# State space layer of a three-layer fp32 block: skip folded into the chunk matrices, a new order of states and outputs, and p @ w_pe of the next gate moved into it

## The chip, the cores and the metric

The kernel is one program on one core of a Trainium2 chip. The metric is device time in microseconds of one execution. Before the change three runs took 3111.47, 3125.9 and 3119.45 us, median 3119.45.

## What is computed

A sequence of 512 tokens with 1024 features passes through a first block (convolutions and gating, a mixture of experts, a gated embedding) and a second block of two layers. The first layer of the second block is a state space layer; it is followed by a feed-forward part and again by a gated embedding. The change touches the state space layer and that gated embedding:

```
def s5_mixer(h, w_in, ..., d_skip, w_glu):
    u = h @ w_in
    ...
    y = ys.transpose(2, 0, 1, 3, 4).reshape(bsz, seqlen, SSM_DIM)
    y = y + d_skip.astype(f32) * u.astype(f32)
    g = jax.nn.gelu(y).astype(h.dtype)
    val, gate = jnp.split(g @ w_glu, 2, axis=-1)
    return val * jax.nn.sigmoid(gate)
...
    x = x + conv_ffn(h, ffn_w_up[i], ffn_conv_w[i], ffn_conv_b[i], ffn_w_down[i])
    gate = jax.nn.sigmoid(rms_norm(x, ple_norm[i]) @ ple_w_gate[i])
    x = x + (p[i] @ ple_w_proj[i]) * gate
```

`ys` is a linear recurrence over time, with a complex diagonal state of 64 per group of 16 features (64 groups).

## The kernel before, in words

**Products.** Features lie on the 128 partitions, the 512 tokens along the free side; `x` is 8 tiles of 128x512. Every fp32 product is made of three passes of rounded operands (`mm3`, L161 to L163): high x high, low x high, high x low. Weights come as strips of 128 output features (512 KB, 128x1024). For a strip SP loads the raw tile (`wr`, L135), ACT makes the high part (`wh`, L148), DVE or POOL (if the strip's `pool` flag is set) subtracts for the low part (`wl`, L150), and PE does 24 matmuls of 128x512. An activation is split in the same way (ACT L117 or L119, DVE L112 or L114).

**Order.** No scheduler moves anything: each engine executes its instructions in the order in which the program calls them. `order` lists all strips of the kernel in the order of use. `next_strip` loads up to `LA_DMA` strips and prepares up to `LA` strips ahead of the one in use. `tick` ends an item of work; `later(n, f)` puts the work of the other engines on that item n items further on. All loads of strips and most other DMAs are issued from the one queue of SP, in order; an issue that waits (for a free buffer, or for data that it writes out) holds all that stand behind it. Raw strips have four buffers (`wr`), `wh` and `wl` three each.

**The state space stage** (`ssm`) works through the list `SSM_ORDER` of items for m = 0 to 7:

- `u m`: one strip of `ssm_w_in`. PE multiplies; DVE scales into `u` (L1470); SP writes it to DRAM (`ud`, L1471) and reads it back in another layout (`U`, L1465).
- `s m`: 32 small matmuls of the matrices `m2` with `U` (L1494, tile `st`). DVE multiplies twice by the table `csd` (L1502, L1503), POOL adds (L1504, L1505), DVE scans (L1511), multiplies twice (L1512, L1513), and DVE and POOL form the states `X` (L1520).
- `o m`: 32 matmuls (tile `yy`, L1530 and L1531) of `m1` with `U` and `m3` with `X`. ACT copies out (`y`, L1540, four pieces), PE turns the tile (`yt`, L1546), DVE adds the skip (L1551), ACT applies gelu (L1555), and the result is split into `yg` (ACT L117, DVE L112).

`m1`, `m2`, `m3` and `csd` are 512, 512, 512 and 256 KB per item, built earlier in the expert stage (`ssm_prep`) and read back from DRAM. Afterwards 16 strips of `w_glu` are multiplied with `yg`.

**The gated embedding** (`ple`) multiplies eight strips of `w_pg` with the normalised `x` and gates p @ w_pe with it: `w_pe` is two strips of four output tiles, each tile 6 matmuls (`pp`). `ple_head` does four tiles between the feed-forward part and the first gate strip, `ple_proj(1)` the other four between gate strips 5 and 6. `ple(i)` for i = 1 is the one after the feed-forward part of the state space layer.

## Time and profile before

| what | value |
|---|---|
| median of three runs | 3119.45 us |
| the profiled execution's own time | 3122.41 us |
| its span, first to last instruction | 3120.6 us |
| PE busy, DVE busy | 94%, 71% |
| ACT busy, POOL busy | 41%, 38% |
| mean granted clock of TensorE | 0.965 of full |
| state space stage, from the first u strip to the first w_glu strip | about 1786 to 1875 us of the span |
| gated embedding after it | about 2326 to 2392 us |

PE stands for matmuls, PEld for weight loads, POOL for GpSimd, SP for the queue that issues most transfers. Busy time of PE is a modelled overlap of pipelined matmuls; a stage is read better from when one group of matmuls starts and the next one starts. A row's bracket says how long the engine was idle before the instruction and what ended that.

### The profile page before, as it was taken

What the parts mean: (1) busy time and instruction counts of PE and PEld (TensorE: products, weight loads), DVE (VectorE), ACT (ScalarE), POOL (GpSimd) and SP (SyncE); (2) the same over time, 40 slices, a digit from 0 to 9 for tenths busy, and PEclk for the clock granted to TensorE, in tenths of its full rate; (3) what the DMA queues carried; (4) which work ended last, traced back from release to release, by engine and by line L of the source; (5) the groups of instructions that cost most, each with busy time, mean ns of one, the idle gap of its engine ahead of it and who ended that gap; (6) DMA issues with size and microseconds to landing.
All of it is one profiled execution on the core that took longest, in us unless ns stands there. A gap on an engine that the chain in (4) does not pass through costs nothing. (4 is left out here: it accounts for less than half of the span.)

```text
span 3120.6 us, 39487 instructions
## 1 busy us (share of the span) xinstructions
PE 2923.9 (94%) x14359; PEld 2456.2 (79%) x14359; DVE 2216.9 (71%) x3786; ACT 1266.7 (41%) x2016; POOL 1183.6 (38%) x1032
## 2 busy tenths in 40 slices
PE   8999988888999999999998989999999998999998
PEld 6677888787888787878877768888877766888886
DVE  7946888995898878787887684565675457566665
ACT  4333256566433333333334533433344345433333
POOL 3224565653248879788886330000011011100001
PEclk9889999999999999999999989999999989999999
DMA  4124344778788888888986283233332211233322
GB/s 138 48 84 150 105 142 163 248 252 305 252 290 304 291 314 299 307 286 305 317 291 221 89 256 103 86 101 98 97 97 88 81 40 49 93 97 101 95 73 96
DMA packets 248891, 534.77 MB, mean 171 GB/s; under 512 B 36671, under 2 KB 129219, under 8 KB 248314
## 3 DMA queue, kind: packets, MB, share of 16 engines
q1 hardware_dynamic: 170570, 343.69, 33.7%
q0 software_dynamic: 38656, 140.74, 13.0%
q10 hardware_dynamic: 39472, 47.84, 4.4%
q8 instruction: 113, 1.85, 0.2%
q14 instruction: 80, 0.66, 0.1%
HBM read 468.75 MB, written 63.44 MB: 171 GB/s over the span
## 5 line engine op out<-in xcount | busy, mean ns | idle before, releaser
L150 DVE TENSOR_TENSOR wl<-wr,wh 128x1024 fp32r<-128x1024 f32 (+2 forms) x453 | 548.7, 1221 | 456.4 <-ACT wh L148 447.6
L148 ACT ACTIVATE wh<-wr 128x1024 fp32r<-128x1024 f32 (+2 forms) x552 | 545.7, 997 | 505.5 <-PE mm L163 209.9
L161 PE MATMUL mm<-xn,wh 128*128 128x512 f32 x1296 | 521.4, 402 | 12.9 <-ACT xn L119 7.6
L163 PE MATMUL mm<-xn,wh 128*128 128x512 f32 x1296 | 512.4, 395 | 5.8 <-DVE xn L114 5.8
L162 PE MATMUL mm<-xn,wl 128*128 128x512 f32 x1296 | 512.8, 396 | 2.0 <-POOL wl L150 1.9
L230 POOL TENSOR_TENSOR accs<-accs,sq 128x512 f32<-128x512 f32 x56 | 86.2, 1540 | 1014.1 <-ACT sq L229 1009.2
L1077 PE MATMUL pv<-wh,A 128*128 128x512 f32 x1536 | 443.2, 402 | 22.5 <-DVE A L112 10.1
L150 POOL TENSOR_TENSOR wl<-wr,wh 128x1024 fp32r<-128x1024 f32 x99 | 241.1, 2436 | 450.4 <-ACT wh L148 439.4
L1077 PEld LDWEIGHTS pv<-wh,A 128*128 128x128 f32 x1536 | 291.8, 193 | 89.0 <-DVE A L112 17.6
L162 PE MATMUL mm<-n,wl 128*128 128x384 f32 x1024 | 348.3, 340 | 13.5 <-DVE wl L150 11.7
L161 PE MATMUL mm<-n,wh 128*128 128x384 f32 x1024 | 352.7, 344 | 0.8 <-ACT gs L703 0.8
L163 PE MATMUL mm<-n,wh 128*128 128x384 f32 x1024 | 347.8, 340 | 3.1 <-DVE n L114 3.1
L161 PEld LDWEIGHTS mm<-xn,wh 128*128 128x128 f32 x1296 | 248.6, 192 | 68.4 <-ACT xn L119 8.1
L163 PEld LDWEIGHTS mm<-xn,wh 128*128 128x128 f32 x1296 | 248.0, 191 | 61.4 <-DVE xn L114 8.6
L162 PEld LDWEIGHTS mm<-xn,wl 128*128 128x128 f32 x1296 | 248.6, 192 | 55.9 <-POOL wl L150 2.3
L1077 PE MATMUL pv<-wl,A 128*128 128x512 f32 x768 | 245.3, 401 | 26.6 <-DVE wl L150 26.6
L117 ACT ACTIVATE A<-ga 128x384 fp32r<-128x384 f32 x128 | 67.3, 525 | 424.6 <-DVE ga L1039 421.4
L998 DVE SCALAR_TENSOR_TENSOR gx<-gx,first 128x1024 f32<-128x1024 f32 x127 | 178.9, 1409 | 59.6 <-DMA gx<-in_exp_v,first 57.9
L162 PEld LDWEIGHTS mm<-n,wl 128*128 128x128 f32 x1024 | 196.0, 191 | 17.8 <-DVE wl L150 13.9
L161 PEld LDWEIGHTS mm<-n,wh 128*128 128x128 f32 x1024 | 196.0, 191 | 5.2 <-issue 1.6
L1077 PEld LDWEIGHTS pv<-wl,A 128*128 128x128 f32 x768 | 145.9, 192 | 67.4 <-DVE wl L150 35.1
L163 PEld LDWEIGHTS mm<-n,wh 128*128 128x128 f32 x1024 | 195.9, 191 | 3.5 <-DVE n L114 3.5
(409 smaller groups left out, 5356.4 us busy)
## 6 DMA issues: line engine op xcount, KB each, us to landing
wr<-in_exp_u SPq DMA_DIRECT2D x128, 512.0 KB
wr<-in_exp_v SPq DMA_DIRECT2D x128, 512.0 KB
wr<-in_w_up SPq DMA_DIRECT2D x88, 512.0 KB
gd<-gb ACTq DMA_DIRECT2D x48, 512.0 KB
G<-gd SPq DMA_DIRECT2D x32, 768.0 KB
wr<-in_w_dn SPq DMA_DIRECT2D x64, 320.0 KB
wr<-in_w_pg SPq DMA_DIRECT2D x24, 512.0 KB
sd<-gs SPq DMA_DIRECT2D x56, 192.0 KB
```

Source lines behind the costliest of these rows:

```text
L117: nc.scalar.activation(hi, src, AF.Copy)
L148: nc.scalar.activation(s.hi, s.raw, AF.Copy)
L150: eng.tensor_tensor(s.lo, s.raw, s.hi.bitcast(F32), ALU.subtract)
L161: t.matmul(ps, wh, xh, start=start, stop=False)
L162: t.matmul(ps, wl, xh, start=False, stop=False)
L163: t.matmul(ps, wh, xl, start=False, stop=stop)
L230: self.later(1, lambda: nc.gpsimd.tensor_tensor(acc, acc, sq, ALU.add))
L998: nc.vector.scalar_tensor_tensor(out=acc, in0=g, scalar=act[:, j : j + 1], in1=acc, op0=ALU.mult, op1=ALU.add)
L1077: nc.tensor.matmul(pv[2 * b + h], a[:, x, o], w[:, h * T : h * T + T], start=(e == 0 and i == 0 and w is s.hi), stop=last)
```

## The change

The skip `d_skip * u` is no longer added by DVE. It is added to the diagonal of the matrices `m1` when these are built: ACT copies only the part of the tile behind the first 16 columns, and DVE adds `eye * d` to the first 16 in two small instructions for each of the 16 parts. Gelu reads the turned tile in PSUM. The low part of `yg` is made by POOL. Outputs come later in the order (three states ahead), the lag of the turning matmuls is 2 items, and the strips of `u3` and `u5` get their low part from POOL.

The eight tiles of p @ w_pe for the gated embedding that follows are made inside the state space stage, as two items `p0` and `p1` of four tiles. ACT copies each tile out (`ppo`), SP writes it to DRAM (`ppd`, L1597 after the change), and `ple` reads the tiles back (`ppk`). The two strips of `w_pe` get their low part from POOL. Both places in the gated embedding where these matmuls stood fall away there.

```
     def plan_ple(self, i):
...
+        if i == 1:
+            self.order += g
+        else:
+            self.order += p[:1] + g[:6] + p[1:] + g[6:]
...
     def ple(self, after, kept=None):
...
+        def fetch(m):
+            if kept is not None and m < 8:
+                self.pp[m] = self.st.tile([P, T], F32, tag="ppk", name=self.name("ppk"), bufs=4)
+                nc.sync.dma_start(self.pp[m], kept[m])
...
         def gate(m):
+            fetch(m + 2)
...
-        for _ in self.ple_proj(1):
+        for _ in self.ple_proj(1) if kept is None else ():
...
-                nc.scalar.copy(o, pk[0:32])
+                nc.scalar.copy(o[:, :, 16:], pk[0:32, :, 16:])
+                for a in range(QP):
+                    V.scalar_tensor_tensor(
+                        out=o[:, a, 0:16], in0=eye, scalar=dT[:, q * QP + a : q * QP + a + 1], in1=pk[0:32, a, 0:16], op0=ALU.mult, op1=ALU.add
+                    )
...
-    YL = 1
+    YL = 2
...
-    SSM_ORDER = "u0 u1 u2 u3 s0 u4 s1 u5 o0 s2 u6 o1 s3 u7 o2 s4 o3 s5 o4 s6 o5 s7 o6 o7"
+    SSM_ORDER = "u0 u1 u2 u3 s0 u4 s1 u5 s2 o0 u6 s3 o1 u7 s4 o2 p0 s5 o3 s6 o4 s7 p1 o5 o6 o7"
...
-            def skip(m, ps):
-                y2 = self.tmp((P, 8, NCH), tag="y2")
-                nc.vector.scalar_tensor_tensor(
-                    out=y2, in0=u[m], scalar=self.v("ssm_d")[:, m : m + 1], in1=ps, op0=ALU.mult, op1=ALU.add
-                )
+            def bend(m, ps):
                 y = self.tmp(tag="yg")
-                nc.scalar.activation(y.rearrange("p (n t) -> p t n", t=8), y2, AF.Gelu_apprx_tanh)
-                self.split(yg[:, m, 0, :], yg[:, m, 1, :], y)
+                nc.scalar.activation(y.rearrange("p (n t) -> p t n", t=8), ps, AF.Gelu_apprx_tanh)
+                hi, lo = yg[:, m, 0, :], yg[:, m, 1, :]
+                nc.scalar.copy(hi, y)
+                self.later(1, lambda: nc.gpsimd.tensor_tensor(lo, y, hi.bitcast(F32), ALU.subtract))
+
+            def project(h):
+                s = self.next_strip()
+                for j in range(4):
+                    ps, m = self.mm(name="pp"), 4 * h + j
+                    for k in range(2):
+                        c = slice((2 * j + k) * P, (2 * j + k + 1) * P)
+                        self.mm3(ps, s.hi[:, c], s.lo[:, c], self.ph[:, k, 0, :], self.ph[:, k, 1, :], k == 0, k == 1)
+                    def keep(ps=ps, m=m):
+                        o = self.tmp(tag="ppo")
+                        nc.scalar.copy(o, ps)
+                        nc.sync.dma_start(ppd[m], o)
+                    self.later(1, keep)
+                    self.tick()
...
+            self.ple_fetch(1)
+            self.later(8, self.ple_load)
             stat(st)
-            la, self.LA_DMA = self.LA_DMA, self.SSM_LA
+            la, self.LA_DMA, self.LA = (self.LA_DMA, self.LA), self.SSM_LA, 3
...
-        self.ple_head()
+        if ple == 2:
+            self.ple_head()
```

**First place: SP's queue behind the write of u5.** `ud<-u` writes u5 and later u6 to DRAM, `m1d`, `m3d` and `m2d` are the chunk matrices, `in_ssm_w_in` is the strip of u7. Before:

```order
L1471 DMA ud<-u_2626_14995 128x512
L135 DMA wr_15354<-m2d 128x1024
L1479 DMA tab_14999<-csd 128x512
L135 DMA wr_15392<-in_ssm_w_in 128x1024
L1465 DMA U_15420<-ud 128x8x64
L135 DMA wr_15437<-m1d 128x8x128
L135 DMA wr_15443<-m3d 128x1024
L1471 DMA ud<-u_2627_14996 128x512
```

After the change the same stretch of SP's queue, up to the first strip of `w_pe`:

```order
L1500 DMA ud<-u_15387 128x512
L1508 DMA tab_15028<-csd 128x512
L135 DMA wr_15399<-m1d 128x8x128
L135 DMA wr_15401<-m3d 128x1024
L135 DMA wr_15437<-in_ssm_w_in 128x1024
L1493 DMA U_15465<-ud 128x8x64
L135 DMA wr_15471<-m2d 128x1024
L1500 DMA ud<-u_15499 128x512
L1508 DMA tab_15028<-csd 128x512
L135 DMA wr_15511<-m1d 128x8x128
L135 DMA wr_15513<-m3d 128x1024
L135 DMA wr_15551<-in_w_pe 128x1024
```

The strip of u7 stood behind one matrix (m2 of s3) and the table; it now stands behind the two matrices of o1 and the table. The matrices of o2 stood ahead of the write of u6 and now stand behind it.

**Second place: SP's queue from the last read of U to the second strip of w_pe.** `ppd<-ppo` writes one tile of p @ w_pe. Before, from the write of u7:

```order
L1471 DMA ud<-u_2628_14997 128x512
L135 DMA wr_15582<-m1d 128x8x128
L1479 DMA tab_14999<-csd 128x512
L135 DMA wr_15619<-m3d 128x1024
L135 DMA wr_15621<-m2d 128x1024
L1465 DMA U_15640<-ud 128x8x64
L135 DMA wr_15663<-m1d 128x8x128
```

After the change, from the last read of U; the write of the last tile of p0 is the one that ends in 15720:

```order
L1493 DMA U_15674<-ud 128x8x64
L1597 DMA ppd<-ppo_15677 128x512
L1597 DMA ppd<-ppo_15696 128x512
L1597 DMA ppd<-ppo_15709 128x512
L1597 DMA ppd<-ppo_15720 128x512
L135 DMA wr_15723<-m1d 128x8x128
L1508 DMA tab_15028<-csd 128x512
L135 DMA wr_15751<-m3d 128x1024
L135 DMA wr_15753<-m2d 128x1024
L135 DMA wr_15788<-in_w_pe 128x1024
```

The matrices of o4 followed the last read of U directly; they now stand behind four writes that wait for the tiles of p0, and the matrix of s7 and the strip of p1 stand behind those.

**Third place: the end of the stage, SP and ACT.** `in_w_glu` are the strips that follow the stage. SP before:

```order
L135 DMA wr_15778<-m3d 128x1024
L135 DMA wr_15780<-m1d 128x8x128
L135 DMA wr_15820<-m3d 128x1024
L135 DMA wr_15855<-in_w_glu 128x1024
L135 DMA wr_15857<-in_w_glu 128x1024
```

SP after the change:

```order
L1597 DMA ppd<-ppo_15944 128x512
L1597 DMA ppd<-ppo_15954 128x512
L135 DMA wr_15957<-m1d 128x8x128
L135 DMA wr_15959<-m3d 128x1024
L135 DMA wr_15984<-in_w_glu 128x1024
L135 DMA wr_15990<-in_w_glu 128x1024
L135 DMA wr_16019<-in_w_glu 128x1024
```

ACT after the change, from the last copy of o6 (`y_16010`) to the first gelu of the last three:

```order
L1569 COPY y_16010<-yy_15992 64x4x4x16
L148 ACTIVATE wh_16015<-wr_15990 128x1024
L148 ACTIVATE wh_16021<-wr_16019 128x1024
L1569 COPY y_16053<-yy_16027 64x4x4x16
L1569 COPY y_16054<-yy_16027 64x4x4x16
L1569 COPY y_16053<-yy_16027 64x4x4x16
L1569 COPY y_16054<-yy_16027 64x4x4x16
L1580 ACTIVATE yg_16068<-yt_16044 128x8x64
```

The last matrices (o7) and the strips of `w_glu` now stand behind the writes of the four tiles of p1, and on ACT the copies of o7 stand behind the high parts of the second and third strip of `w_glu`.

## Rows read from the trace of the kernel before

**Rows 1.** The page, chain that ended last: share of the span by engine.

```profile
PE 34%; DVE 5%; issue 1%; ACT 1%; POOL 0%; DMA 0%; SPq 0%; ACTq 0%; POOLq 0%; DVEq 0%
```

**Rows 2.** Windows: us, busy us of PE, PEld, DVE, ACT, POOL; PEclk, DMA share, GB/s.

```profile
1800.00:1820.00 20.00, 17.39 (x153) 14.37 (x152) 17.83 (x22) 4.66 (x8) 8.11 (x12) 0.91 0.74 214
1820.00:1840.00 20.00, 19.19 (x189) 15.75 (x188) 17.30 (x23) 8.29 (x15) 6.77 (x12) 0.92 0.92 275
1840.00:1860.00 20.00, 13.13 (x207) 12.38 (x208) 16.92 (x24) 9.57 (x19) 7.82 (x15) 0.83 1.03 320
1860.00:1876.00 16.00, 11.03 (x92) 9.57 (x93) 12.60 (x16) 7.12 (x14) 4.81 (x7) 0.57 0.57 209
```

**Rows 3.** Groups of DVE from 1797 to 1876: count, busy us, mean ns, idle before.

```profile
L112 DVE TENSOR_TENSOR yg<-yg,yg 128x512 fp32r<-128x512 f32 x6 | 5.8, 964 | 0.1
L1551 DVE SCALAR_TENSOR_TENSOR y<-u,vec,yt 128x512 f32<-128x512 f32 x7 | 5.2, 736 | 1.5 <-PE yt L1546 1.5
```

**Rows 4.** Timeline of DVE: start, us, instruction; idle time before in brackets.

```profile
1827.80 1.23 DVE L150 TENSOR_TENSOR wl<-wr,wh 128x1024 fp32r<-128x1024 f32 x1 [0.89 <-ACT wh L148]
...
1829.55 1.19 DVE L1470 TENSOR_TENSOR u<-mm,rstd 128x512 f32<-128x512 f32 x1
```

**Rows 5.** Timeline of SP: start, us, and the transfer issued.

```profile
1819.24 0.32 SPq L1471 DMA_DIRECT2D ud<-u  x1
...
1820.57 0.42 SPq L135 DMA_DIRECT2D wr<-in_ssm_w_in  x1
```

**Rows 6.** Timeline of ACT: start, us, idle time before in brackets.

```profile
1785.68 0.58 ACT L254 COPY rstd<-px 128x512 f32<-128x512 f32 x1 [1.66 <-PE px L252]
...
1826.71 1.06 ACT L148 ACTIVATE wh<-wr 128x1024 fp32r<-128x1024 f32 x1 [2.46 <-DMA wr<-in_ssm_w_in]
...
1873.39 1.29 ACT L1540 COPY y<-yy 64x256 f32<-64x256 f32 x4 [3.52 <-PE yy L1531]
```

**Rows 7.** Timeline of PE in the state space stage.

```profile
1810.88 0.45 PE L1530 MATMUL yy<-wr,U 128*64 128x128 f32 x4
...
1812.68 1.15 PE L1494 MATMUL st<-U,wr 128*64 128x64 f32 x32
...
1816.44 1.11 PE L1546 MATMUL yt<-ident,y 64*128 64x64 f32 x8 [2.61 <-ACT y L1540]
...
1829.62 0.50 PE L161 MATMUL mm<-xn,wh 128*128 128x512 f32 x1
...
1861.88 0.44 PE L1531 MATMUL yy<-wr,X 128*64 128x128 f32 x1 [0.80 <-POOL X L1520]
...
1869.68 0.45 PE L1531 MATMUL yy<-wr,X 128*64 128x128 f32 x1 [4.11 <-POOL X L1520]
...
1875.12 0.50 PE L161 MATMUL mm<-yg,wh 128*128 128x512 f32 x1
```

**Rows 8.** Tile wl on POOL, whole kernel: ns shortest, median, longest; first and last start.

```profile
L150 POOL TENSOR_TENSOR wl<-wr,wh x99: 2333/2398/3215, 21.5 to 2634.7; 128x1024 fp32r<-128x1024 f32 x99
```

**Rows 9.** Timeline of PE in the gated embedding after the feed-forward part.

```profile
2326.16 0.50 PE L161 MATMUL pp<-ph,wh 128*128 128x512 f32 x1
...
2343.32 0.95 PE L240 MATMUL px<-ones,accs 128*128 128x1 f32 x8
...
2369.28 0.40 PE L161 MATMUL pp<-ph,wh 128*128 128x512 f32 x1
...
2374.56 0.39 PE L163 MATMUL pp<-ph,wh 128*128 128x512 f32 x1
```

**Rows 10.** Timeline of DVE there.

```profile
2332.28 1.72 DVE L150 TENSOR_TENSOR wl<-wr,wh 128x1024 fp32r<-128x1024 f32 x1
...
2336.22 1.62 DVE L114 SCALAR_TENSOR_TENSOR xn<-x,vec,xn 128x512 fp32r<-128x512 f32 x2
```

**Rows 11.** Where m1 is built: tile m1o, and the timeline of ACT behind it.

```profile
L1375 ACT COPY m1o<-m1p x16: 344/346/362, 941.6 to 1680.3; 32x256 f32<-32x256 f32 x16
...
942.99 1.06 ACT L148 ACTIVATE wh<-wr 128x1024 fp32r<-128x1024 f32 x1 [1.06 <-issue]
```

More of the change, by code (lines that the diff above doesn't have):

```diff
@@ L1120, in ple_head, with ple @@
             pass
-    def ple(self, after):
+    def ple(self, after, kept=None):
         nc = self.nc
@@ L1140, in gate @@
             return f
-        self.few = True
+        if kept is not None:
+            self.pp = {}
+            for m in range(2):
+                fetch(m)
+        self.few = kept is None
         self.norm_stat(st)
@@ L1182, in ssm_prep @@
         den, x1, x2 = s(), s(), s()
+        eye, dT = s((32, 16)), s((32, 32))
         f = s((P, 2, 32))
@@ L1439, in plan_ssm @@
                 self.order.append(Strip(I["ssm_w_in"][m], KT))
+                self.order[-1].pool = m in (3, 5)
+            elif what == "p":
+                self.order.append(Strip(I["w_pe1"][m], KT))
+                self.order[-1].pool = True
             elif what == "s":
@@ L1457, in ssm @@
             ud = self.dp.tile([8, P, 8, NCH], F32, name="ud")
-            u = [self.loc((P, 8, NCH), tag=f"u{m}") for m in range(8)]
             U = {}
+            ppd = self.ppd = self.dp.tile([8, P, T], F32, name="ppd")
             yg = self.ap.tile([P, KT, 2, T], F32R, tag="xn", name="yg", bufs=2)
@@ L1566, in ssm @@
                     self.lin(xn, p_u(m))
+                elif what == "p":
+                    project(m)
                 else:
@@ L1673, in ffn @@
                 last = b == 22
-                if last:
+                if last and ple == 2:
                     self.ple_fetch(ple)
```

17 lines of the change are left out of this document (10 added, 7 removed).

## The prediction, made before the changed kernel ran

> **What bounds the kernel now.** I read the chain that ended last first: PE holds the largest part of it, DVE and waits the rest [rows 1]. So a place counts where PE stops, and the windows find one at the state space stage: PE is busy 17.39 of 20 us, 19.19 of 20, 13.13 of 20 and 11.03 of 16, and its granted clock falls from 0.91 to 0.57 of full; in the same windows the transfers use 0.74, 0.92, 1.03 and 0.57 of the DMA engines, 320 GB/s in the third [rows 2]. The timeline of PE then shows what it waits for: the output items stop for `X`, 0.80 us at 1861.88 and 4.11 us at 1869.68, and these two stand 7.8 us apart [rows 7]. That is the pace of DVE, which makes the states and, between them, the skip (0.74 us each) and the low part of `yg` (0.96 us) [rows 3]. Two things are near the bound in this stage, DVE and the transfers. The change relieves the first and loads the second.
>
> **What it removes from DVE.** Eight skips of 0.736 us are 5.9 us, eight low parts of 0.964 us 7.7 us [rows 3], the low parts of u3 and u5 at 1.23 us 2.5 us [rows 4]: 16 us of some 65 us busy in the four windows (17.83 + 17.30 + 16.92 + 12.60) [rows 2]. By itself this would shorten 7.8 us per state to about 6. What PE would then wait for next decides.
>
> **What it adds there.** PE gets 8 tiles of 6 matmuls. Two such blocks of four tiles stand in the gated embedding now; the second runs from 2369.28 to 2374.56 plus 0.23, 5.5 us [rows 9], so 11 us. The transfers get 8 writes of 256 KB and 2 strips of 512 KB; the two loads of p come before the stage's transfers, and I cost them at nothing there. ACT's eight copies out of PSUM (0.58 us each [rows 6]) lie in a queue that is half empty (9.57 of 20 us [rows 2]), except where said below. Gelu from PSUM: the only difference is where it reads; I take it as equal.
>
> **The new path through the stage, step by step.** For a transfer I use 1.64 us per 512 KB (0.524 MB at 320 GB/s [rows 2]) for all that is issued ahead of it, plus 2.5 us. I fitted the 2.5: the strip of u7 landed at 1826.71 [rows 6], 7.4 us after the write of u5 was issued at 1819.24 [rows 5], with 1.5 MB (3 x 1.64 us) in between, itself included.
>
> 1. *u7.* Splitting p on DVE delays the write of u5 by two subtractions, some 1.3 us by the size of a `wl` of 1.23 us [rows 4], to 1820.5. The strip of u7 now stands behind two matrices instead of one: 4 x 1.64 + 2.5 = 9.1 us, landing at 1829.6 instead of 1826.7. High part 1.06 [rows 6], low part 1.23 [rows 4]: PE starts at 1831.9 instead of 1829.62 [rows 7] and ends at 1837.4.
> 2. *o2 and p0.* DVE's product of u6 (1.19 [rows 4]) is queued behind that low part, SP's write of u6 behind the product, at 1833.1, and the matrices of o2 and the first strip of `w_pe` behind the write: 9.1 us, 1842.2. ACT 1.06, POOL 2.40 [rows 8]: 1845.7. Four tiles of 5.5 us and one turn of 1.11 [rows 7]: p0 ends at 1852.3.
> 3. *o4, s7 and p1.* The write of the last tile of p0 waits for ACT's copy, 1853.2. Behind it on SP wait m1 and m3 of o4 (with the table 3 x 1.64 + 2.5, 1860.6), m2 of s7 (1862.3) and the second strip of `w_pe` (1863.9). PE has done s5, o3 and s6 by 1856.4 (1.15, 1.8, 1.15 us [rows 7]) and stands for about 4 us. ACT and POOL make the strip ready at 1867.4, p1 with one turn ends at 1874.0.
> 4. *o7 and w_glu.* SP again waits for the copy of the last tile, 1874.9; m1 and m3 of o7 land at 1881.5, where o5 and o6 are long done. The output takes 1.8 us. Three strips of `w_glu` need 3 x 1.64 more, 1886.4, and ACT's copies of o7 (1.29 [rows 6]) stand behind the high part of the third (1.06). With the last turn (1.11) the first `w_glu` matmul starts at 1889.9, now 1875.12 [rows 7]: +15.
>
> With the last window's pace (209 GB/s at 0.57, 367 at full use [rows 2]) the four waits shrink by 4 us together: +11. I take **+13**, in the middle, since the rows hold both paces. The Trainium skill (DMA: Bandwidth & Descriptors, section Anatomy of one DMA — SWDGE (gpsimd) path) fits one transfer, on another issuing path, as 2.0 us plus bytes over 436 GB/s; by it the stage would lose only about 5 us and the forecast would be 3118. The row gives 7.4 us for what the fit makes 5.6, so I stay with the row.
>
> **What falls away in the gated embedding.** The second block, 5.5 us, goes fully: strips follow each other there and PE sets the pace. The first, from 2326.16, does not: the first gate strip ends at 2343.32 [rows 9], and its operands come from DVE, the last of them at 2336.22 + 1.62 [rows 10]. One of three low parts goes (1.72 us [rows 10]), so the operands come at 2336.1; behind the seventh PE still has some 6 us, the strip ends about 2341.8: 1.5 us gained, with 0 and 7 as ends. The tiles are read back two strips ahead, 11 us, where 256 KB need 2.5 + 0.8 us: nothing; without that lead 3 us once. **-7** in all.
>
> **The building of m1** gets 32 small DVE instructions. Nearest row: ACT's copy of the whole tile, 0.35 us [rows 11], so 11 us at most; ACT's transfers now wait for DVE, but ACT stood 1.06 us before its next strip [rows 11]. Ends 0 and 11; **+1**, by that cover. If DVE were later than the gap, PE would wait for strips.
>
> **Sum.** +13 - 7 + 1 = +7 on the profiled execution's 3122.4, 3129.4. That execution stands 3.0 above the median of the runs; I take that off: **3126**. A measurement of this kernel can tell about 0.5% from no change (3103.9 to 3135.0), so this is no change.
>
> **Rivals.**
>
> *The queue keeps up (0.18).* The transfers run ahead as far as the buffers allow, and the stage ends when its bytes are through. For: they fill 0.92 to 1.03 of the engines already [rows 2], so a queue without gaps would need little more time. Against: the writes of p0 and p1 stand in SP's one queue. The stage would then end about 1870: -5 - 7 + 1 = -11, **3108**.
>
> *PE stays at its low clock (0.14), the slower side.* On the path of steps 2 to 4 PE has 16.1 us of its own (p0 and p1 with their turns 6.6 each, o7 1.8, the last turn 1.1). PE fell to a mean of 0.57, 1.2 GHz for most of it, in the window where it was busy 11.03 of 16 us [rows 2], 69%; in steps 2 to 4 it works about 65% of the time. At 0.57 these 16.1 us become 28.2: +12, **3138**. It decides from a mean clock of about 0.65 (+9). Against: with 66% in the third window the clock was 0.83.
>
> *POOL holds DVE off (0.10).* The low part of `yg` took 0.96 us on DVE in the mean, behind POOL's share of `X` [rows 3]. Between s5 and the last `X` POOL gets two strips of 2.40 and five halves of 1.2 [rows 8], 10.8 us. If DVE stood still for all of it, then, at the present 7.8 us per state from 1853.5, the last `X` would come at 1887.7, 6 us after the matrices of o7: **3132**. The Trainium skill (SBUF — State Buffer, section SBUF: two separate sides) says that the two share one pair of ports as an exclusive lock, held for a whole instruction; no row here shows a full stop.
>
> *ACT's transfers for m1 wait long (0.08).* A further microsecond in each of 16 parts: **3141**.
>
> The forecast itself keeps 0.50, with 3116 to 3136 as its own range. **The range** 3106 to 3144 takes in all four rivals and leaves out some 0.2: a clock still lower, or a stage that ends before 1868. Faster by over 0.5% needs the first rival and more: 0.08. Slower by over 0.5%: most of the low clock's and m1's cases and the upper tail of the others, 0.22. The rest, 0.70, is no change.
>
> **What would show it.** Each step has a row: PE's first matmul of u7 near 1832, p0 waiting for POOL's `wl` near 1845, an o4 that waits for m3, SP waiting for ACT's copies, o7 waiting for its matrices, and w_glu starting near 1888 (all counted from the same start). In the gated embedding, no `pp` and a first strip that waits for `xn`. It is wrong if the skipless DVE lets o7 start before 1870, if SP never waits for a copy, or if the time moves outside these two stages.

## Result and the profile after

| | before | after |
|---|---|---|
| median, us | 3121.35 (6 runs, 3111.47 to 3125.9) | 3140.09 (6 runs, 3135.36 to 3153.05) |
| profiled execution, own time / span | 3122.4 / 3120.6 | 3153.05 / 3151.3 |

The ratio is 1.0063, 95% interval 1.0041 to 1.0085: the change makes the kernel slower, by 18.7 us in the medians. The whole range of the prediction, 3106 to 3144, holds this. The range of its forecast alone, 3116 to 3136, does not, and neither does "no change within 0.5%", the case it gave 0.70; the interval begins just below that, at 0.41%.

The profiled execution of the changed kernel is the slowest of its six, 13 us above their median. To see where that sits I cut both traces at TensorE's first product of each stage. The windows of the changed kernel, from the last gathered product of the expert stage on (the expectations call it the peer stage; us, busy us and count of PE, PEld, DVE, ACT, POOL; granted clock, DMA share, GB/s):

```profile
1715.20:1804.70 89.50, 79.92 (x369) 65.17 (x369) 57.35 (x69) 48.90 (x73) 37.85 (x24) 0.95 0.22 71
1804.70:1907.10 102.40, 84.68 (x770) 68.82 (x769) 66.15 (x80) 39.51 (x70) 40.66 (x54) 0.92 0.79 248
1907.10:1996.90 89.80, 89.80 (x386) 74.11 (x386) 31.98 (x36) 33.06 (x44) 12.08 (x9) 0.97 0.31 99
1996.90:2359.80 362.90, 362.85 (x1602) 298.78 (x1600) 223.69 (x303) 138.35 (x186) 5.00 (x4) 1.00 0.30 92
2359.80:2432.30 72.50, 62.50 (x253) 48.48 (x254) 49.58 (x53) 33.17 (x47) 16.82 (x12) 0.91 0.34 117
2432.30:3151.30 719.00, 693.58 (x3236) 551.38 (x3234) 417.36 (x749) 290.83 (x548) 47.63 (x25) 0.99 0.26 81
```

The stage and the second gated embedding ("gate", defined below) of the kernel before:

```profile
1786.30:1875.10 88.80, 73.54 (x723) 62.51 (x721) 73.98 (x92) 32.93 (x59) 27.55 (x46) 0.85 0.82 253
...
2326.20:2400.40 74.20, 69.41 (x301) 56.39 (x302) 48.72 (x55) 35.23 (x49) 17.57 (x12) 0.98 0.31 99
```

The stages are: the first gated embedding and the norm up to the first in-strip ("start"), the state space stage up to the first product of `w_glu` ("stage"), `w_glu` ("GLU"), the feed-forward part ("FFN"), the second gated embedding with the head of the attention up to its norm's statistic ("gate"), and the rest. The same cuts in every kernel that ran, in us; "sum" is all of them, and the last columns are the ratio of the runs' times to the kernel before, with its 95% interval. The stages are those of one profiled execution of each kernel:

| kernel | start | stage | GLU | FFN | gate | rest | sum | ratio | interval |
|---|---|---|---|---|---|---|---|---|---|
| before | 85.7 | 88.8 | 87.2 | 363.9 | 74.2 | 720.2 | 1420.0 | | |
| after | 89.5 | 102.4 | 89.8 | 362.9 | 72.5 | 719.0 | 1436.1 | 1.0063 | 1.0041 to 1.0085 |
| p_back | 88.1 | 89.1 | 87.2 | 364.2 | 72.6 | 720.5 | 1421.6 | 1.0030 | 1.0005 to 1.0054 |
| fold_only | 85.6 | 85.3 | 87.2 | 363.9 | 72.7 | 719.9 | 1414.6 | 1.0007 | 0.9984 to 1.0031 |
| order_only | 87.3 | 87.1 | 87.2 | 364.0 | 75.6 | 721.2 | 1422.5 | 0.9986 | 0.9967 to 1.0004 |
| fold_send | 85.9 | 85.8 | 88.7 | 364.0 | 72.7 | 719.4 | 1416.4 | 1.0026 | 1.0008 to 1.0044 |
| fold_gate | 89.4 | 87.1 | 87.2 | 364.1 | 73.7 | 718.4 | 1419.8 | 0.9998 | 0.9980 to 1.0016 |
| la_late | 85.9 | 103.4 | 89.5 | 362.9 | 74.0 | 720.3 | 1436.0 | 1.0069 | 1.0044 to 1.0093 |
| ppd_act | 89.5 | 104.1 | 89.0 | 362.9 | 73.7 | 720.5 | 1439.6 | 1.0065 | 1.0041 to 1.0089 |
| p_early | 89.4 | 101.8 | 88.5 | 362.9 | 71.0 | 719.5 | 1433.1 | 1.0052 | 1.0030 to 1.0073 |
| p_thin | 89.5 | 99.6 | 89.6 | 362.9 | 74.0 | 721.1 | 1436.7 | 1.0079 | 1.0059 to 1.0100 |
| gate_first | 91.9 | 101.5 | 88.6 | 362.9 | 66.7 | 717.6 | 1429.1 | 1.0044 | 1.0026 to 1.0063 |
| sig_psum | 89.5 | 102.2 | 89.7 | 362.9 | 71.0 | 720.0 | 1435.2 | 1.0064 | 1.0042 to 1.0086 |
| m1_plain | 89.5 | 102.8 | 89.5 | 362.9 | 74.0 | 721.2 | 1439.8 | 1.0055 | 1.0032 to 1.0078 |

The sums tell what the medians alone can't: behind the last gathered product the change costs 16.1 us, start +3.8, stage +13.6, GLU +2.6, FFN -1.0, gate -1.7, rest -1.2. The other 14.6 us by which the two profiled spans differ lie ahead of that product, at 1700.6 before and 1715.2 after. It came anywhere from 1689.9 (gate_first) to 1719.4 us (fold_send): so most of the spread of the runs (17.7 us over six runs of the change) seems to lie there. The stages repeat better, but not exactly. Fold_only, fold_send and fold_gate have the same instructions in the state space stage and took 85.3, 85.8 and 87.1 us there; the change, m1_plain, gate_first and sig_psum also share theirs and took 101.5 to 102.8. A few microseconds are therefore read below from the stages, not from medians, and a difference of up to 2 us between two single traces is not taken as shown.

**The steps of the state space stage.** The first product of the in-strips came at 1804.70, before at 1786.29, so 18.41 us are taken off to compare with the prediction's times. PE's timeline of the changed kernel (start, us, instruction, idle time before in brackets):

```profile
1849.93 0.50 PE L162 MATMUL mm<-xn,wl 128*128 128x512 f32 x1 [0.76 <-DVE wl L150]
...
1863.55 0.50 PE L162 MATMUL pp<-ph,wl 128*128 128x512 f32 x1 [1.94 <-POOL wl L150]
...
1876.90 0.40 PE L1559 MATMUL yy<-wr,U 128*64 128x128 f32 x2 [1.63 <-DMA wr<-m1d]
...
1878.92 0.45 PE L1560 MATMUL yy<-wr,X 128*64 128x128 f32 x1 [1.61 <-DMA wr<-m3d]
...
1885.61 0.50 PE L162 MATMUL pp<-ph,wl 128*128 128x512 f32 x1 [1.10 <-POOL X L1545]
...
1899.48 0.45 PE L1560 MATMUL yy<-wr,X 128*64 128x128 f32 x1 [0.88 <-DMA wr<-m3d]
...
1907.11 0.79 PE L161 MATMUL mm<-yg,wh 128*128 128x512 f32 x1
```

u7 goes on at 1831.5 (forecast 1831.9), p0 at 1845.1 with GpSimd's low part (1845.7), o4 waits for m3 until 1860.5 (1860.6), p1 goes on at 1867.2 (1867.4), o7 has its m3 at 1881.1 (1881.5), and `w_glu` starts at 1888.7 (1889.9 by the steps, 1888.1 with the 13 us taken). In the kernel before, PE waited in this stage 4.9 us for `X` [rows 7], 6.2 us for ACT's copies `y` and 2.8 us for the matrices m1 and m3. In the change it no longer waits for `X` at an output; it waits 8.6 us for m1 and m3 and 2.0 us for the copies.

### The profile page after: what moved, and what is told of

It reads as the page before. It is cut to its first block, busy times and chain, and to the rows that moved or that the text cites. A ratio compares the mean times of both kernels' runs of the same rounds, so it can differ in the third digit from the quotient of the medians.

```text
span 3151.3 us, 39587 instructions
## 1 busy us (share of the span) xinstructions
PE 2934.2 (93%) x14359; PEld 2455.3 (78%) x14359; DVE 2204.8 (70%) x3799; ACT 1268.5 (40%) x2024; POOL 1201.2 (38%) x1044
## 4 chain that ended last, share of the span: by engine, by line
PE 45%; DVE 25%; DMA 10%; issue 8%; POOL 6%; ACT 4%; SPq 1%; ACTq 1%; DVEq 0%; POOLq 0%
PE mm L161 12%; PE mm L163 12%; PE mm L162 12%; DVE wl L150 4%; DMA gx<-in_exp_v,first 4%; PE pv L1077 4%; ACT wh L148 2%; DMA gx<-in_rows_u,first 2%; DVE cacc L442 2%; DVE gh L907 2%; POOL gx L974 1%; DMA wr<-in_exp_v 1%; DVE oh L893 1%; DVE ga L1039 1%; DVE gx L998 1%
## 5 line engine op out<-in xcount | busy, mean ns | idle before, releaser
L150 DVE TENSOR_TENSOR wl<-wr,wh 128x1024 fp32r<-128x1024 f32 (+2 forms) x449 | 540.0, 1213 | 475.0 <-ACT wh L148 470.7
L150 POOL TENSOR_TENSOR wl<-wr,wh 128x1024 fp32r<-128x1024 f32 x103 | 250.9, 2437 | 470.7 <-ACT wh L148 463.3
L1077 PEld LDWEIGHTS pv<-wh,A 128*128 128x128 f32 x1536 | 292.7, 193 | 91.9 <-DVE A L112 14.6
```

The lines of the kernel that those rows point to most:

```text
L150: eng.tensor_tensor(s.lo, s.raw, s.hi.bitcast(F32), ALU.subtract)
L1077: nc.tensor.matmul(pv[2 * b + h], a[:, x, o], w[:, h * T : h * T + T], start=(e == 0 and i == 0 and w is s.hi), stop=last)
```

## Experiments

**1. Projections put back: p_back.**

```diff
-    SSM_ORDER = "... o2 p0 s5 o3 s6 o4 s7 p1 o5 o6 o7"
+    SSM_ORDER = "... o2 s5 o3 s6 o4 s7 o5 o6 o7"
-            self.ple(norm_into(V("attn_norm")), self.ppd)
+            self.ple(norm_into(V("attn_norm")))
```

(and `plan_ple`, `ple_head`, the load of p as before).

> The change with p @ w_pe1 put back into the gated embedding, everything else kept (skip in the matrices, gelu from PSUM, low part on GpSimd, states three ahead, three strips prepared ahead). State space stage, from the first product of its in-strips to the first product of w_glu: 88.8 us before, 102.4 us in the change. Theory (the two projections lengthen this stage by more than the gated embedding saves): the stage is 88 to 92 us, the gated embedding is 2 us longer than in the change, and the median is 3121 to 3130 us. Rival 1 (building the first matrix, with the skip added on VectorE in each of 16 parts, costs some 15 us before the stage starts): the first product of the stage still comes 12 to 18 us later than in the kernel before (1786.3 us) and the median is 3133 us or more. Rival 2 (the order with states three ahead is what costs, not the projections): the stage is 97 us or longer.

Stage 89.1 us, median 3132.4 against 3124.2. The stage bears the theory out: the projections cost 13.3 us in it. The gate is 72.6 us, as in the change, not 2 us longer, and the start is still 88.1. The first product of the stage came at 1788.6, 2.3 us later than before and not 12, so rival 1 falls on its first part, though the median is near its 3133, and rival 2 falls with the stage. The median lies above the theory's 3130; the stages behind the last gathered product sum to only 1.6 us more than before, so the rest of it is not located.

**2. The fold alone: fold_only.** The kernel before with skip in the matrices, gelu from PSUM and the low part on GpSimd: p_back with `YL = 1`, two strips ahead, no `pool` flags, and the old `SSM_ORDER`.

> The kernel before with the fold alone: skip in the matrices, gelu from PSUM, low part of its result on GpSimd; order, depth of preparation and the projections as before. Theory (the fold takes 16 VectorE operations out of the stage and costs next to nothing in the peer stage): the state space stage is 83 to 88 us against 88.8 before, the median 3113 to 3121 us. Rival 1 (the fold's building costs some 15 us in the peer stage): the first product of the stage comes near 1800 us and the median is 3130 us or more. Rival 2 (the stage is held by transfers and GpSimd and the VectorE work was hidden): the stage stays within 1 us of 88.8 and the median within 4 us of the kernel before.

Stage 85.3, start 85.6, sum 1414.6: 5.4 less than before, of it 3.5 in the stage. The two other kernels with the same stage (fold_send, fold_gate) took 85.8 and 87.1 there, so the fold's gain in the stage is 1.7 to 3.5 us. The median, 3127.1 against 3124.2, does not show it: 1.0007 with an interval from -0.16% to +0.31%. Rival 2 falls by the stage. Rival 1 does not quite hold (median under 3130, first product of the stage at 1795.8) and is not excluded by it either. Whether the fold is a gain as a whole stays open.

**3. One part of the fold left out: m1_plain.**

```diff
-                nc.scalar.copy(o[:, :, 16:], pk[0:32, :, 16:])
-                for a in range(QP):
-                    V.scalar_tensor_tensor(out=o[:, a, 0:16], in0=eye, ...)
+                nc.scalar.copy(o, pk[0:32])
```

> The change with the first matrix copied to SBUF whole, by one ScalarE copy per part as before: the 32 additions of the skip on VectorE are gone, so the skip is left out of the result. Theory (the addition costs at most 1 us in all; the later start of the state space stage in the profile of the change, 1804.7 us against 1786.3, is the spread of the gathering stretch of one run, since its median lies 13 us under that run): the median stays within 4 us of the change's 3140. Rival (the transfers of the first matrix, which now wait for VectorE, hold ScalarE's queue in each of 16 parts): the stage starts 10 us or more sooner than 1804.7 and the median falls to 3126 us or less.

3140.1, the same as the change, as the theory has it. The stage started at 1795.9, 8.8 us sooner than in the trace of the change; kernels that have the additions start it anywhere from 1781.8 to 1805.3, so that says nothing of them. ACT's waits in the expert stage, for the changed kernel, fold_only and m1_plain (us in total, times, longest):

```profile
ACT wh L148 <- DVE m1o L1396: 18.8, 12, 1.9
```

```profile
ACT wh L148 <- DVE m1o L1392: 25.8, 15, 3.5
```

```profile
ACT wh L148 <- ACT m1o L1394: 12.8, 14, 1.0
```

ACT does wait 6 to 13 us more in 16 parts, and no time of the kernel goes with it as far as the medians can tell (their intervals are 7 us either way).

**4. m1's transfers one background piece later: fold_send.**

```diff
-            return load, bbs, [..., table, m1], [m2, store]
+            return load, bbs, [..., table, m1], [m2, send, store]
```

(`send` holds the two transfers that were the end of `m1`).

> The kernel before with the fold alone, and the two transfers of each part of the first matrix issued one background piece later, behind those of the second matrix. Theory (in the peer stage ScalarE, and with it the next strip's high part, waits for the addition of the skip on VectorE: 18.8 to 25.8 us in 11 to 15 waits with the fold, 10.0 to 12.8 us without it; this costs some 5 us): the waits behind this line fall under 5 us, the peer stage is 4 to 8 us shorter in the median than with the fold alone, and the median is 3115 to 3123 us against 3127. Rival (the difference between the stages' sums and the medians is the spread of the gathering stretch): the median stays within 3 us of 3127.

The waits behind this line went, but the time did not fall: 3134.2 us against 3129.4 of the kernel before, 1.0026. The theory that they cost 5 us falls. ACT's high parts waited for other transfers instead, for one 38.1 us behind the writes of m3 against 27.5 in fold_only. The rival's 3127 did not come either.

**5. The order without the projections: order_only.** p_back with two strips ahead and all low parts on DVE.

> The fold with the change's order (states three items ahead, outputs transposed two items later), without the projections, with two strips prepared ahead and all low parts on VectorE as before. State space stage: 85.3 us with the old order, 89.1 us with the new order and three strips ahead. Theory (the order itself costs: a state moved ahead of an output delays the output's chain and the loads behind it): 88 to 90 us, and the stage's start 85.6 us after the last gathered product. Rival (the third strip ahead and GpSimd's low parts cost it): 84 to 86 us.

Stage 87.1, between the two: 1.8 us above fold_only and 2.0 below p_back. That is below the theory's 88 to 90 and above the rival's 84 to 86. Fold_gate, with the old order, took 87.1 as well, so a cost of the order is not shown, nor is one of the third strip ahead; both together are at most some 4 us. The start was 87.3, not 85.6; there the norm's 16 small matmuls on PE (L252) took 3.57 us against 2.05 before, mostly at the lower of the two clock levels (1.2 and 2.4 GHz).

**6. Three strips ahead only behind the first two: la_late.**

```diff
-            la, self.LA_DMA, self.LA = (self.LA_DMA, self.LA), self.SSM_LA, 3
+            la, self.LA_DMA, self.LA = (self.LA_DMA, self.LA), self.SSM_LA, self.LA
             self.lin2(xn, p_u(0), p_u(1))
+            self.LA = 3
```

> The change with the preparation of three strips ahead switched on only behind the first two in-strips of the state space stage. Theory (with three ahead from the first strip, ScalarE transposes one more strip, which waits for a buffer until TensorE has finished the first strip's seven blocks, ahead of the table load and square root of the norm's statistic; the kernels with it start the stage 88.0 to 89.4 us after the last gathered product, those without it 85.6): the start comes 85.6 to 87 us after the last gathered product, and the stage stays at 101 to 103 us. Rival (the fetch of the projections' input or the granted clock at the stage's head costs it): the distance stays at 89 us or more.

("Transposes one more strip" means that ACT makes the high part of one more strip.) Start 85.9, 3.6 us less, as the theory has it; the stage took 103.4, 1.0 more. The sum (1436.0) and the ratio (1.0069) are no lower than the change's: the other stages gave the 3.6 us back in this trace. ACT's timeline around the norm's statistic, of the changed kernel:

```profile
1796.70 1.06 ACT L148 ACTIVATE wh<-wr 128x1024 fp32r<-128x1024 f32 x1 [5.48 <-PE mm L163]
1797.78 1.28 ACT L242 ACT_TABLE_LOAD   x1
1799.07 0.26 ACT L242 ACTIVATE rc<-px,eps 128x4 f32<-128x4 f32 x1
```

and of la_late:

```profile
1782.83 1.28 ACT L242 ACT_TABLE_LOAD   x1
1789.08 0.26 ACT L242 ACTIVATE rc<-px,eps 128x4 f32<-128x4 f32 x1 [4.97 <-PE px L240]
```

In the change the fourth high part (1796.70) waits until PE has finished with a buffer, and the table load and the square root stand behind it in ACT's queue; in la_late the table is loaded while PE works. PE pays for it in the change:

```profile
1801.27 2.08 PE L252 MATMUL px<-ident,fr 128*128 128x128 f32 x8 [2.11 <-DVE fr L2011]
```

PE is idle for 2.11 us, against 0.18 in la_late, and the matmuls behind that run at the low clock (2.08 us for the first eight; in la_late 1.16).

**7. Writes of the projections from ACT's queue: ppd_act.**

```diff
-                        nc.sync.dma_start(ppd[m], o)
+                        nc.scalar.dma_start(ppd[m], o)
```

> The change with the eight writes of the projections issued from ScalarE's queue, right behind the copies, and not from SyncE's. Theory (SyncE waits for the copies, 15.8 us in eight waits, and the matrices of the fifth and the eighth output and w_glu's strips stand behind): the fifth output's first product follows the seventh state at once, TensorE's waits for its matrices (1.6 and 1.6 us, and 2.4 and 0.9 us at the eighth output) are gone or under 1 us in all, and the stage takes 95 to 98 us against 102.4. Rival 1 (the transfers are bound by their rate, so an earlier issue lands no earlier): the stage stays at 101 us or more. Rival 2 (ScalarE's issues delay its strips and copies by as much): SyncE's waits go, and TensorE's waits for ScalarE grow by 4 us or more.

104.1 us: no gain. The theory, which is the reason given in steps 3 and 4 of the prediction, falls as the only reason. In the change SP did wait for the copies (us in total, times, longest):

```profile
SPq L1597 <- ACT ppo L1596: 15.8, 8, 4.5
```

In ppd_act it no longer does, but it waits as long, for other things:

```profile
SPq L135 <- PE pp L163: 14.0, 1, 14.0
SPq L1508 <- DMA ppd<-ppo: 7.1, 1, 7.1
```

The first is o7's m1. The chunk matrices m1 are loaded straight into the buffers of high parts. The last eight strips use three buffers of high parts in turn, o2, p0, o3, o4, p1, o5, o6, o7: o7's matrix is loaded into the buffer of p1's high part and can't be issued before PE is through with p1. In the change itself p1's last matmul ended 0.6 us before its last copy (1892.1 and 1892.7 us), so the buffer and the write held o7's m1 for nearly the same time. The second stands ahead of o4's m3. In the trace the transfers of both queues count their landings on eight counters in turn, and SP's read of the table waits for the landing of a write of the projections that used its counter before it (issued at 1846.20, landed at 1851.57). Counted from the start of the stage, SP issued o4's m3 at 67.6 us against 69.0 in the change, and o7's m1 at 89.8 against 88.5. Since hardly anything was issued earlier, the run does not test rival 1, the rate of the transfers. Over the whole stage the transfers use 0.79 of the DMA engines in the change and 0.82 before, which speaks against it but does not settle it. Rival 2 falls: PE's waits for ACT's high parts and copies grew from 3.4 to 5.9 us, by less than 4.

**8. The second projection earlier: p_early.**

```diff
-    SSM_ORDER = "... o2 p0 s5 o3 s6 o4 s7 p1 o5 o6 o7"
+    SSM_ORDER = "... o2 p0 s5 o3 p1 s6 o4 s7 o5 o6 o7"
```

> The change with the second projection two places earlier in the state space stage, ahead of the seventh state and the fifth output. Theory (a projection's strip holds one of three buffers of the high and low parts, and the last output's matrices are loaded into the second projection's; the place sets how long TensorE waits, on top of 11 us of its work): TensorE's wait for the last output's matrices (2.4 and 0.9 us) goes, the second projection's own wait grows, and the stage takes 99 to 102 us against 102.4. Rival (the write of the projections on SyncE alone sets the waits): the wait for the last output's matrices goes wholly and the stage takes 96 us or less.

101.8, so the rival's 96 or less did not come. The wait of o7 for its matrices is gone, and o4 and the last outputs wait longer instead (2.08 us for m1 at o4; 2.41 and 2.25 us for ACT's copies of `y`). The place moves the waits; the 0.6 us by which the stage is shorter lie within the spread of kernels with one and the same stage.

**9. A third of the projections' matmuls: p_thin.** Of six matmuls per tile two stay; strips, parts, copies and writes stay.

> The change with 16 of the 48 matmuls of the two projections in the state space stage: for each output block the high and the low part of one of its two input blocks with the high part of the input alone, so the other 32 products are left out of the result; strips, their high and low parts, copies and writes stay. The 48 matmuls keep TensorE busy for 13.9 us in the stage, two thirds of it is 9.2 us. Theory 1 (the projections cost their matmul time, which lies on the path of the stage): the stage takes 92 to 95 us against 102.4 with all and 89.1 without projections. Theory 2 (the projections cost by their strips, which fill the transfers and hold buffers the outputs' matrices need): 99 to 103 us. Between them, both.

99.6. The 16 matmuls left keep PE busy for 6.99 us, where the 48 took 13.86: 6.9 us of work gone, not 9.2, make the stage 2.8 us shorter, at the lower edge of theory 2's time. What the projections cost here is, for the larger part, not their matmuls but what comes with them: strips in the buffers and queues, copies and writes, which this run leaves in and does not tell apart.

**10. Sigmoid into PSUM: sig_psum.** In the second gated embedding DVE's multiplication reads the sigmoid from the PSUM bank of its product.

```diff
-                nc.scalar.activation(t, t, AF.Sigmoid)
+                sg = t if kept is None else ps
+                nc.scalar.activation(sg, t, AF.Sigmoid)
-                    nc.vector.tensor_tensor(t, t, self.pp[m], ALU.mult)
+                    nc.vector.tensor_tensor(t, sg, self.pp[m], ALU.mult)
```

> The change, but in the second gated embedding the sigmoid is written into the PSUM bank of its product, so that the multiplication by the fetched projection reads one operand from PSUM, as it does in the kernel before, and not both from SBUF. Theory (the multiplication is held while GpSimd adds the squares: 1.78 us against 0.68 before, which lengthens the loop of VectorE and ScalarE per strip from 5.84 to 6.56 us): the multiplication takes 0.7 us throughout, the loop 5.8 to 5.9 us, the next attention starts 3 to 5 us sooner against the start of the gated embedding, and the median is 3135 to 3138 us. Rival (the loop is set by the ScalarE transposition of strips and not by the held multiplication, or the longer hold of the PSUM bank stops TensorE): the loop stays at 6.4 us or more and the median within 1 us of the change's 3140.

First the loop that is meant. DVE's timeline over one strip of the second gated embedding, of the kernel before:

```profile
2366.11 1.22 DVE L150 TENSOR_TENSOR wl<-wr,wh 128x1024 fp32r<-128x1024 f32 x1 [1.65 <-ACT wh L148]
2367.25 0.74 DVE L114 SCALAR_TENSOR_TENSOR xn<-x,vec,xn 128x512 fp32r<-128x512 f32 x1
2367.92 0.68 DVE L1135 TENSOR_TENSOR pt<-pt,pp 128x512 f32<-128x512 f32 x1
2368.63 1.07 DVE L1136 TENSOR_TENSOR x<-x,pt 128x512 f32<-128x512 f32 x1
2369.62 0.68 DVE L1131 TENSOR_TENSOR pt<-mm,rstd 128x512 f32<-128x512 f32 x1
2371.95 1.23 DVE L150 TENSOR_TENSOR wl<-wr,wh 128x1024 fp32r<-128x1024 f32 x1 [1.65 <-ACT wh L148]
...
2376.14 1.23 DVE L150 TENSOR_TENSOR wl<-wr,wh 128x1024 fp32r<-128x1024 f32 x1 [2.96 <-ACT wh L148]
```

of the changed kernel:

```profile
2400.29 1.23 DVE L150 TENSOR_TENSOR wl<-wr,wh 128x1024 fp32r<-128x1024 f32 x1 [1.65 <-ACT wh L148]
2401.44 0.74 DVE L114 SCALAR_TENSOR_TENSOR xn<-x,vec,xn 128x512 fp32r<-128x512 f32 x1
2402.10 1.78 DVE L1146 TENSOR_TENSOR pt<-pt,ppk 128x512 f32<-128x512 f32 x1
2403.91 0.69 DVE L1147 TENSOR_TENSOR x<-x,pt 128x512 f32<-128x512 f32 x1
2404.52 0.69 DVE L1142 TENSOR_TENSOR pt<-mm,rstd 128x512 f32<-128x512 f32 x1
2406.85 1.23 DVE L150 TENSOR_TENSOR wl<-wr,wh 128x1024 fp32r<-128x1024 f32 x1 [1.65 <-ACT wh L148]
```

and of sig_psum:

```profile
2397.47 1.23 DVE L150 TENSOR_TENSOR wl<-wr,wh 128x1024 fp32r<-128x1024 f32 x1 [1.65 <-ACT wh L148]
2398.61 0.75 DVE L114 SCALAR_TENSOR_TENSOR xn<-x,vec,xn 128x512 fp32r<-128x512 f32 x1
2399.27 0.69 DVE L1147 TENSOR_TENSOR pt<-mm,ppk 128x512 f32<-128x512 f32 x1
2399.99 1.07 DVE L1148 TENSOR_TENSOR x<-x,pt 128x512 f32<-128x512 f32 x1
...
2403.31 1.23 DVE L150 TENSOR_TENSOR wl<-wr,wh 128x1024 fp32r<-128x1024 f32 x1 [1.65 <-ACT wh L148]
```

Once a strip DVE makes the gate's product (0.68), waits while ACT does the sigmoid and the next high part (1.65), and makes the low part and the rest. In the strips beside which the next norm's input is written, as here, this takes 5.84 us a strip before, 6.56 in the change, 5.84 in sig_psum; in the two strips ahead of them it takes 4.8 in all three. PE needs 24 matmuls at 0.227 us, 5.44 us. So before the change already the loop of DVE and ACT was slower than PE in those strips; the last row of the kernel before stands only 4.19 us behind the one ahead of it, because there PE is busy with the second projection. The change slowed the loop by 0.72 us a strip: its multiplication reads both operands from SBUF, the projection being fetched there. Three of the eight multiplications took 1.78 us, each beside an addition of squares on POOL:

```profile
2401.54 1.79 POOL L230 TENSOR_TENSOR accs<-accs,sq 128x512 f32<-128x512 f32 x1 [5.37 <-ACT sq L229]
```

With one operand in PSUM it takes 0.68 us beside such a POOL instruction, and the addition to `x` behind it, with both operands in SBUF, takes 1.07 instead of 0.69. The Trainium skill (SBUF — State Buffer, section SBUF: two separate sides) says that a DVE operation with two SBUF inputs and a GpSimd operation that reads SBUF exclude each other for a whole instruction; these rows agree, the held one ending 0.55 us after POOL's. From the statistic of the gate's norm to that of the attention's, sig_psum took 54.1 us, where the six kernels with the held multiplication and the old order took 55.7 to 57.2. So the hold cost 1.6 to 3.1 us there, at best the lower end of the 3 to 5 expected, and the median (3143.8) doesn't show it. The gate as a whole tells less: 71.0 us, but p_early, which keeps the hold, took 71.0 too.

**11. Another order in the gated embedding: gate_first.** The product and sigmoid of a strip are issued ahead of the multiplication and addition of the strip before it.

```diff
-                    self.later(1, lambda: after(m))
+                    self.later(1, lambda: self.later(0, lambda: after(m)))
-                self.later(1, mul)
+                self.later(1, lambda: self.later(0, mul))
```

> The change with another order of work inside each gated embedding: the product with the norm's factor and the sigmoid of a strip are issued ahead of the multiplication and addition of the strip before it, and the next input is written one place later. Theory (the two projections' 11 us of TensorE work taken out of the second gated embedding were not saved, because VectorE and ScalarE wait for each other once a strip: the product, the sigmoid, the next high part, the next low part, then the rest, 6.56 us a strip in the change against 5.44 us of TensorE work): the loop falls to TensorE's 5.4 to 5.6 us a strip, the time from the norm's statistic of the second gated embedding to that of the attention falls from 55.7 to 50 to 53 us, the head of the state space stage comes 1 to 3 us sooner behind the last gathered product, and the median is 3132 to 3137 us against the change's 3140 or 1.004 to 1.005 times the kernel before. Rival (the loop's time is the sum of VectorE's own work, and the held operations only move): 6.2 us a strip or more, no gain over 1 us.

Gate 66.7 us against 72.5, from statistic to statistic 51.4 against 55.7, median 3135.7, 1.0044: as the theory has it there, though the interval of the ratio overlaps the change's. DVE's rows in the second gated embedding now stand 5.5 to 5.6 us apart, PE's pace:

```profile
2370.78 1.47 DVE L150 TENSOR_TENSOR wl<-wr,wh 128x1024 fp32r<-128x1024 f32 x1 [1.46 <-ACT wh L148]
...
2376.30 1.54 DVE L150 TENSOR_TENSOR wl<-wr,wh 128x1024 fp32r<-128x1024 f32 x1 [1.46 <-ACT wh L148]
...
2381.88 1.53 DVE L150 TENSOR_TENSOR wl<-wr,wh 128x1024 fp32r<-128x1024 f32 x1 [1.46 <-ACT wh L148]
```

The expected gain at the start did not come: it is 2.4 us longer, since in the first gated embedding the last inputs are now written later and PE waits 2.03 us for one where it waited 0.61.

**12. Fold and this order together: fold_gate.** fold_only with the edit of 11.

> The kernel before with the fold (skip in the matrices, gelu from PSUM, low part on GpSimd) and the order of work inside the gated embeddings of gate_first; no projections moved. Theory: state space stage 85 to 86 us against 88.8; the second gated embedding 52 to 54 us against 55.5 to 57.1 (its second projection still stands in it); the first 1 to 3 us shorter; sum of the stages behind the last gathered product 1410 to 1413 us against 1420; median 0.996 to 0.999 of the kernel before. Rival (the fold's building gives it back in the peer stage): 1.000 or above.

0.9998 of the kernel before: a miss. The start took 89.4, in part for the reason just told, and the stage 87.1. The gate, in which the projections still stand, took 73.7, from statistic to statistic 56.5 and not 52 to 54: PE is busy for 69.25 of the 73.7 us there, so the order of the loop has little to give. No version was shown to beat the kernel before; order_only, at 0.9986, has 1 inside its interval.

## Why the prediction was right and wrong

1. *The state space stage, +13 taken: +13.6.* Every step of the path came within 1.2 us of its row. Of the parts, the fold takes 1.7 to 3.5 off, the order, the third strip ahead and GpSimd's low parts together add at most some 4, and the projections 13.3. The fit of 2.5 us plus all that is issued ahead, taken from one strip of the trace before, held; the other figure weighed there, 5 us for the stage, did not. The reason in steps 3 and 4 was not the only one, though: with SP free of the copies (ppd_act) the stage is no shorter, because a buffer of the projections' strips (for o7) and a counter of landings (for o4) hold the same matrices about as long. That these came out at the same times as the copies is luck. So is part of the 13: the steps gave 15, and 2 were taken off as the middle between two paces.
2. *The gated embedding, -7: this term failed.* "The second block, 5.5 us, goes fully: strips follow each other there and PE sets the pace." PE did not set the pace. The rows that say so stood in the trace before: `wl` to `wl` 5.84 us against PE's 5.44. While PE worked on the projection, DVE and ACT caught up; without it PE runs ahead of them, and stops at the attention's head for `xn`:

```profile
2415.36 0.50 PE L163 MATMUL mm<-xn,wh 128*128 128x512 f32 x1 [0.78 <-DVE xn L114]
...
2419.03 0.80 PE L163 MATMUL mm<-xn,wh 128*128 128x512 f32 x1 [2.72 <-DVE xn L114]
...
2422.17 0.79 PE L163 MATMUL mm<-xn,wh 128*128 128x512 f32 x1 [1.29 <-DVE xn L114]
...
2425.18 0.80 PE L163 MATMUL mm<-xn,wh 128*128 128x512 f32 x1 [1.36 <-DVE xn L114]
```

   Before, there were two waits there:

```profile
2390.03 0.50 PE L163 MATMUL mm<-xn,wh 128*128 128x512 f32 x1 [0.29 <-DVE xn L114]
...
2393.03 0.62 PE L163 MATMUL mm<-xn,wh 128*128 128x512 f32 x1 [2.03 <-DVE xn L114]
```

   By the rows of the gate in the result section, the 48 matmuls gone are 10.9 us at 0.227 us each. PE's idle time grew from 4.8 to 10.0 us, and the matmuls that stayed took 4.0 us more, at a granted clock of 0.91 instead of 0.98. So of 10.9 us 1.7 were left. The gate took 71.0 to 74.0 us in the six kernels with the projections moved and the old order of the gate (mean 73.2; the change, la_late, ppd_act, p_early, p_thin, m1_plain), and 72.6 to 75.6 in the five with them in it (mean 73.6; before, p_back, fold_only, order_only, fold_send): 11 us of PE's work were worth 0.4. Gate_first shows that the loop was the cause: with it removed, the gate is 66.7. Against fold_gate (73.7), which has that order and the projections in the gate, this is 7.0 us less: the -7 is right where DVE and ACT keep up. The 1.5 us forecast for the first block came only in part: from the gate's first product to its norm's statistic (the row at 2343.32, which the prediction took for the end of the first gate strip) it took 17.2 us before and 17.0 in the change at a granted clock of 0.90, and 15.3 in p_early and gate_first, where the granted clock was 1.00.
3. *The start, not in the sum: +3.8.* The prediction puts no price on the third strip prepared ahead, and none of its steps looks at ACT's queue at the head of the stage: the third strip ahead puts one more high part, with a wait for a buffer, in front of the norm's table load and square root. La_late, which switches it on later, has a start of 85.9.
4. *GLU, not in the sum: +2.6.* PE enters `w_glu` from the waits at o7 (2.43 and 0.88 us for its matrices, 2.04 for ACT's copies) at the low level. The first 6 us of `w_glu`, after and before:

```profile
1907.10:1913.10 6.00, 6.00 (x16) 4.74 (x16) 0.00 (x0) 5.48 (x7) 3.84 (x3) 0.53 0.40 155
```

```profile
1875.10:1881.10 6.00, 6.00 (x28) 4.98 (x27) 2.11 (x4) 4.40 (x5) 0.00 (x0) 1.00 0.09 36
```

   16 matmuls where 28 went: at a clock of 0.53, mostly 1.2 GHz, 12 matmuls of 0.227 us are 2.7 us late. It is not tied to o7's matrices alone: in p_early, where that wait is gone, `w_glu` took 88.5 us, and in fold_send, which moves no projection, 88.7. Nor does a wait always bring it: in the kernel before, PE waited 4.11 us for the last `X` [rows 7] and `w_glu` began at 1.00. What decides between the two is open. This is the rival of the low clock, at another place and a fifth of its price; inside the stage the granted clock was higher than before (0.92 against 0.85).
5. *The building of m1, +1.* Not told apart from zero: m1_plain lies at 1.0055, the change at 1.0063, and their intervals would hide a few microseconds.
6. *The rivals.* The queue did not keep up (3108), POOL's holds did not move the last `X` behind o7's matrices (3132), and no microsecond in each of 16 parts is seen lost to m1 (3141). A hold did come in the stage, but PE did not wait for `X` after it. A multiplication that took 0.69 us elsewhere took 2.69 beside POOL's low part of p1's strip and ended 0.55 us after it:

```profile
1882.65 2.91 POOL L150 TENSOR_TENSOR wl<-wr,wh 128x1024 fp32r<-128x1024 f32 x1 [0.52 <-ACT wh L148]
...
1883.42 2.69 DVE L1541 TENSOR_TENSOR t<-z,tab 128x512 f32<-128x512 f32 x1
```

   The time measured lies near that of the low clock (3138), but not by that rival's path, the stage: PE lost time to the low level at the start (some 1.7 us), in `w_glu` (2.7) and in the gate (up to 4.0).

7. *The signs.* SP did wait for the copies, and o7 started at 1879.8 us on the prediction's scale, not before 1870. By the third sign, time that moves outside the two stages, the prediction was wrong in part: it moved by +3.8 in the start, +2.6 in GLU, -1.0 in FFN (362.9 us in all eight kernels with the projections moved, 363.9 to 364.2 in the others; the reason was not followed) and -1.2 in the rest, which is within its spread (717.6 to 721.2). None of the rivals had terms 2 to 4, some 12 us together, so that the total stayed in the range is in part luck.

With what was measured the sum is 13.6 + 3.8 + 2.6 - 1.0 - 1.7 - 1.2 = +16.1 where I had +7; the medians give +18.7, and the rest is within the spread of the time ahead of the last gathered product.

## What to carry to other kernels

Before work is taken off an engine, look at the distance between two like rows of the engines that feed it, not only at its own gaps: here 5.84 us against 5.44 said that TensorE was not the bound of that loop, though it hardly ever stood still. A strip that is moved into another stage takes a buffer and a place in every queue there, and these can cost more than its matmuls (here 13.3 us for two strips; without two thirds of the matmuls the stage was only 2.8 us shorter). Removing one wait of a queue shows little where a second one ends at the same time. More preparation ahead is a queue of its own: ask what stands behind the instruction that now waits for a buffer.

## What had not been expected of the hardware

- DVE's multiplication of two SBUF tiles took 1.78 us beside a POOL addition of 1.79 us, and 0.68 us with one of the operands in PSUM. In all three cases it ended 0.55 us after the addition: a hold, not a slower pace.
- After waits of 2.43, 0.88 and 2.04 us TensorE went on at the low level into full work, and `w_glu` began with 16 matmuls in 6 us instead of 28; at the attention's head matmuls took 0.80 us instead of 0.50 behind the waits. In other kernels `w_glu` began at full clock behind a wait of 4.1 to 5.7 us.
